# A two-layer trunk in split float32: one 512-column matmul for both activation parts, and the FFN in two sweeps

## The chip, the cores and the metric

The kernel runs on one core of a Trainium2 chip. Its time is the device time of one execution in microseconds. Three runs of the kernel before gave 978.88 us as their median (978.57 to 980.99). The profile comes from one execution, whose span on the core is 975.6 us. Engines are named as in the profile: PE is TensorE, PEld its weight loads, DVE is VectorE, ACT is ScalarE, POOL is GpSimd, SP is SyncE.

## What is computed

A residual stream `h` of 256 tokens and 1,024 channels goes through two layers. Each has a gated FFN (SwiGLU, 2,816 hidden units), a mixer, a second FFN, and a gated per-layer input (PLE). The mixer of layer 0 is a gated linear recurrence over 1,280 channels, that of layer 1 a causal pooling with windows of 2, 4, 8 and 16 tokens. A last norm follows. All is float32:

```python
for i in range(DEPTH):
    h = h + 0.5 * swiglu(rms_norm(h, ffn1_norm[i]), ffn1_w_gate[i], ffn1_w_up[i], ffn1_w_down[i])
    hn = rms_norm(h, mix_norm[i])
    m = rglru_mixer(hn, ...) if i % 2 == 0 else pool_mixer(hn, ...)
    h = h + m
    h = h + 0.5 * swiglu(rms_norm(h, ffn2_norm[i]), ffn2_w_gate[i], ffn2_w_up[i], ffn2_w_down[i])
    gate = jax.nn.sigmoid(rms_norm(h, ple_norm[i]) @ ple_w_gate[i])
    h = h + gate * (p[i] @ ple_w_proj[i])
return rms_norm(h, final_norm)
```

Here `swiglu(x)` is `(silu(x @ w_gate) * (x @ w_up)) @ w_down`.

## The kernel before

**Layout and precision.** Channels lie on partitions, tokens along the free axis. `h` is four tiles of [128, 2, 256], each a pair of channel tiles. The weights come from DRAM as 329 units, [128, 1024] float32 each, in the order in which `stream_order` lists them. A unit holds eight 128x128 blocks; `load` (L251) brings it in on SP's queue, seven units ahead of its use. `split` then makes two fp32r parts of it, `hl`: ScalarE copies the rounded high part (L262) and VectorE subtracts it from the weights for the low part (L263), four units ahead. The activations are split in the same way: `Norm.put` scales `h` by the norm's weights on ScalarE for the high part (L310) and takes the low part on VectorE (L311). Only the gates of the recurrence (`ri`) use float32 itself, which TensorE does in two passes.

**Products.** A product of a weight block `wh + wl` with activations `xh + xl` is three matmuls of 256 columns, all added up in one PSUM region, in `Bank.mm3` (L284 is where `mm` issues them):

```python
def mm3(self, o, wh, wl, xh, xl):
    self.mm(o, wh, xh)
    self.mm(o, wh, xl)
    self.mm(o, wl, xh)
```

The weights are the stationary side, so each of the three has a weight load (PEld). A result for two channel tiles, [128, 2, 256] float32, fills one PSUM bank. There are two PSUM pools of four banks: `gu` for results that are read soon, `acc` for sums that stay.

**Norms.** The norm's scale by token is found beside the products, which don't need it: `rstd_tokens` adds up the squares with matmuls of one column against `ones` (`ss`, L331), VectorE finds 1/sqrt in ten small steps (L341 to L351), `spread` makes two diagonal tiles `dg` (L367) and multiplies them by `ones` (L368) to have the scale on all partitions. ScalarE's squares (L319) are added on GpSimd (L324) before. `project_all` runs several outputs at once, first the lower half of the contraction for each, then the upper half, and places the sums and the spread between its units: `sums_at` and `spread_at` count units from its start.

**An FFN.** The 2,816 hidden units are 11 pairs of tiles, `p`. The first two pairs of gate and up go through `project_all`, four outputs of two units each. Then for every `p` from 2 on: the down products of `p - 2` into four `acc` banks, then gate and up of `p`, 48 matmuls each; so the down products lie between those of gate and up. `evac` reads the gate's bank on VectorE times the scale (L450), takes tanh on ScalarE, multiplies by the up bank (L453, L454), and splits the result into `hid` (L456, L457). At the end every `acc` bank is scaled and added to `h`, and the next norm's `put` follows.

**Around them.** The recurrent mixer projects two branches (`xb`, `gb`) with the same products, in the order of `LRU_FIRST` and `LRU_STEPS`; the step "y1", whose last instruction is `ytp` (L683), has to end before the last products of `lru_out` (`accl`). The pool mixer multiplies tokens by weights (`v`), waits for the norm's scale to split `v` into `vhl`, and multiplies by the pooling matrices (`po`). The PLE projection (`proj`, results `pp`) is written last there and uses the `acc` pool. `keep_warm` (L231) issues products that nobody reads, at the start and before the last spread. The order on each engine is made by the scheduler from the order of the code; `high_priority` blocks come ahead of what is written before them.

## Time and profile before

| | |
|---|---|
| time, median of 3 runs | 978.88 us (978.57 to 980.99) |
| span of the profiled execution | 975.6 us |
| PE busy | 960.1 us, 98% |
| PEld busy | 952.3 us, 98% |
| DVE busy | 652.3 us, 67% |
| ACT busy | 490.8 us, 50% |
| POOL busy | 55.1 us, 6% |
| granted PE clock | at least nine tenths of full in all 40 slices |
| DMA | 173.63 MB, 178 GB/s mean |
| chain that ended last | PE 65%, issue 21%, DVE 9%, ACT 3% |

The profiled execution has no separate time beside its span; the median of the runs stands 3.3 us above that span. Busy times of PE and PEld are those of instructions that overlap each other: a matmul of 256 columns shows 283 ns of duration while the next one starts some 120 ns after it. What one costs is therefore read from the distance of starts, or from a whole stretch and its count. In the chain, one piece is a run of instructions of one line and operand, with its start, its length and how many they are. "Issue" in the chain is time in which an engine waits for nothing that the profile shows.

### The profile page before, as it was taken

Reading aid. Unit: us, or ns where it says so; the run is one execution under the profiler, and the core shown is the slowest. Engines: PE = TensorE matmul, PEld = TensorE weight load, DVE = VectorE, ACT = ScalarE, POOL = GpSimd, SP = SyncE. Lnnn points to the kernel's source line nnn. Section 1 sums busy time; section 2 is a strip of 40 time slices with the busy share of each in tenths; the row PEclk is TensorE's granted clock in tenths of the full one; section 3 lists DMA queues with packets and bytes.
Section 4 is the critical chain, followed back from the end, with each engine's and each line's share of the span. In section 5 each row is a group of like instructions: output and inputs, shape, how many; then the busy total and the mean of one; then the engine's idle time right before and its main releaser. Section 6 shows DMA issues by size and latency. Waiting matters only on the chain.

```text
span 975.6 us, 18712 instructions
## 1 busy us (share of the span) xinstructions
PE 960.1 (98%) x7888; PEld 952.3 (98%) x7888; DVE 652.3 (67%) x853; ACT 490.8 (50%) x634; POOL 55.1 (6%) x48
## 2 busy tenths in 40 slices
PE   9999999999999999999999999999989999999997
PEld 9999999999999999999998999999989999999996
DVE  7956555597977755655579855555679755555685
ACT  7544444468785443544456444444448444434443
POOL 1000000023101000000021000000011000000020
PEclk9999999999999999999999999999999999999999
DMA  8865556554435665566545656565524765655611
GB/s 294 282 213 184 184 178 192 171 177 175 152 108 169 203 203 173 194 193 185 179 123 185 203 180 192 164 204 182 178 95 157 240 192 169 200 189 176 191 45 44
DMA packets 49188, 173.63 MB, mean 178 GB/s; under 512 B 5584, under 2 KB 6224, under 8 KB 49104
## 3 DMA queue, kind: packets, MB, share of 16 engines
q1 hardware_dynamic: 48960, 172.29, 54.7%
q8 instruction: 61, 1.00, 0.4%
q14 instruction: 23, 0.19, 0.1%
q10 hardware_dynamic: 144, 0.15, 0.1%
HBM read 171.37 MB, written 1.05 MB: 177 GB/s over the span
## 4 chain that ended last, share of the span: by engine, by line
PE 65%; issue 21%; DVE 9%; ACT 3%; DMA 0%; POOL 0%; DVEq 0%; ACTq 0%; POOLq 0%
PE up0ffn L284 13%; PE gate0ffn L284 13%; PE acc0ffn L284 12%; PE up1ffn L284 6%; PE gate1ffn L284 6%; PE acc1ffn L284 6%; DVE hl L263 3%; DVE x L311 2%; PE x L284 2%; PE accl L284 1%; PE ri L284 1%; PE ple L284 1%; ACT hl L262 1%; PE b L284 1%; PE xb L284 1%
## 5 line engine op out<-in xcount | busy, mean ns | idle before, releaser
L263 DVE TENSOR_TENSOR hl<-raw,hl 128x1024 fp32r<-128x1024 f32 (+1 forms) x326 | 385.6, 1200 | 238.5 <-ACT hl L262 238.5
L262 ACT ACTIVATE hl<-raw 128x1024 fp32r<-128x1024 f32 (+1 forms) x326 | 331.9, 1035 | 408.3 <-issue 102.5
L284 PE MATMUL gate1ffn<-x,hl 128*128 128x256 f32 x1056 | 132.6, 283 | 2.4 <-DVE x L311 2.4
L284 PE MATMUL gate0ffn<-x,hl 128*128 128x256 f32 x1056 | 132.2, 283 | 0.6 <-ACT hl L262 0.5
L284 PEld LDWEIGHTS gate1ffn<-x,hl 128*128 128x128 f32 x1056 | 128.9, 192 | 3.5 <-DVE x L311 3.2
L284 PE MATMUL up1ffn<-x,hl 128*128 128x256 f32 x1056 | 132.0, 283 | 0.0
L284 PE MATMUL up0ffn<-x,hl 128*128 128x256 f32 x1056 | 131.3, 283 | 0.0
L284 PEld LDWEIGHTS gate0ffn<-x,hl 128*128 128x128 f32 x1056 | 128.8, 192 | 1.3 <-ACT hl L262 0.7
L284 PE MATMUL acc0ffn<-hid,hl 128*128 128x256 f32 x1056 | 129.0, 282 | 0.0
L284 PEld LDWEIGHTS up1ffn<-x,hl 128*128 128x128 f32 x1056 | 128.9, 192 | 0.0
L284 PEld LDWEIGHTS up0ffn<-x,hl 128*128 128x128 f32 x1056 | 128.6, 192 | 0.0
L284 PE MATMUL acc1ffn<-hid,hl 128*128 128x256 f32 x1056 | 128.6, 281 | 0.0
L284 PEld LDWEIGHTS acc0ffn<-hid,hl 128*128 128x128 f32 x1056 | 126.8, 188 | 0.2
L284 PEld LDWEIGHTS acc1ffn<-hid,hl 128*128 128x128 f32 x1056 | 126.8, 188 | 0.0
L324 POOL TENSOR_TENSOR sacc<-sq,sq 128x512 f32<-128x512 f32 x9 | 14.5, 1609 | 838.7 <-ACT sq L319 838.7
L311 DVE SCALAR_TENSOR_TENSOR x<-h,vt,x 128x256 fp32r<-128x256 f32 x64 | 48.8, 802 | 7.0 <-ACT x L310 7.0
L284 PE MATMUL ple<-x,hl 128*128 128x256 f32 x384 | 47.6, 284 | 0.0
L284 PEld LDWEIGHTS ple<-x,hl 128*128 128x128 f32 x384 | 46.5, 192 | 0.2
L456 ACT ACTIVATE hid<-gs 128x512 fp32r<-128x512 f32 x44 | 27.8, 632 | 16.4 <-DVE gs L454 16.3
L310 ACT ACTIVATE x<-h,vt 128x256 fp32r<-128x256 f32 x64 | 28.5, 499 | 5.9 <-DMA vt<-vec 2.7
L454 DVE TENSOR_TENSOR gs<-th,gs 128x512 f32<-128x512 f32 x44 | 30.4, 692 | 1.4
L457 DVE TENSOR_TENSOR hid<-gs,hid 128x512 fp32r<-128x512 f32 x44 | 30.1, 684 | 0.0
(132 smaller groups left out, 683.3 us busy)
## 6 DMA issues: line engine op xcount, KB each, us to landing
raw<-w SPq DMA_DIRECT2D x320, 512.0 KB, 4.2
raw<-w SPq DMA_DIRECT2D x7, 256.0 KB, 4.6
h<-xT SPq DMA_DIRECT2D x4, 256.0 KB, 6.2
out<-hg SPq DMA_DIRECT2D x3, 256.0 KB, 2.8
raw<-w SPq DMA_DIRECT2D x1, 288.0 KB, 2.6
raw<-w SPq DMA_DIRECT2D x2, 128.0 KB, 4.7
out<-hg SPq DMA_DIRECT2D x2, 128.0 KB, 2.0
vt<-vec ACTq DMA_DIRECT2D x1, 148.0 KB, 4.6
```

The source lines that it names most:

```text
L262: nc.scalar.activation(hl[:, 0, c], raw[:, c], AF.Copy)
L263: nc.vector.tensor_tensor(hl[:, 1, c], raw[:, c], hl[:, 0, c].bitcast(F32), op=ALU.subtract)
L284: nc.tensor.matmul(o, lhsT, rhs, start=self.first, stop=self.left == 0, skip_group_check=True)
L310: nc.scalar.activation(xt[:, 0, c], h[:, c], AF.Copy, scale=g)
L311: nc.vector.scalar_tensor_tensor(xt[:, 1, c], h[:, c], g, xt[:, 0, c].bitcast(F32), op0=ALU.mult, op1=ALU.subtract)
L324: nc.gpsimd.tensor_tensor(acc, self.acc, sq, op=ALU.add)
L454: nc.vector.tensor_tensor(gs, th, gs, op=ALU.mult)
L456: nc.scalar.activation(hid[:, 0], gs, AF.Copy)
L457: nc.vector.tensor_tensor(hid[:, 1], gs, hid[:, 0].bitcast(F32), op=ALU.subtract)
```

## The change

**The pair.** A new class `Pair` takes the place of `Bank` for all split products but those of the pool mixer. Its PSUM tile is [128, 2, 2, 256], two banks; for each of the two channel tiles one half is for the high activations and one for the low ones. The high weights meet both activation parts in one matmul of 512 columns, and the low weights meet the high activations in one of 256 columns, which goes into the second half. `join` adds the two halves afterwards: a ScalarE copy of one half and a VectorE addition of the other. The counts: 2,512 products that were three matmuls are now two; 135 joins; VectorE's instructions go from 809 to 946, ScalarE's from 622 to 748.

```diff
-        def mm3(self, o, wh, wl, xh, xl):
-            self.mm(o, wh, xh)
-            self.mm(o, wh, xl)
-            self.mm(o, wl, xh)
+    class Pair:
+        def __init__(self, name, products):
+            self.ps = psum([P, 2, 2, S], name)
+            self.left = [products, products]
+            self.first = [True, True]
+        def mm3(self, m, wh, wl, x):
+            self.left[m] -= 1
+            nc.tensor.matmul(self.ps[:, m, 1], wl, x[:, 0], start=self.first[m], stop=False, skip_group_check=True)
+            nc.tensor.matmul(self.ps[:, m], wh, x, start=False, stop=self.left[m] == 0, skip_group_check=True)
+            self.first[m] = False
+    def join(out, ps, lo):
+        nc.scalar.activation(lo, ps[..., 1, :], AF.Copy)
+        nc.vector.tensor_tensor(out, ps[..., 0, :], lo, op=ALU.add)
```

**PSUM and the norms.** One PSUM pool `ps` of four tiles (two banks each at most) takes the place of the two. `project_all` now has three outputs, since each is a pair; the fourth goes through the new `project_one`, alone. The marks move with it.

```diff
-    gup = ctx.enter_context(tc.tile_pool(name="gu", bufs=4, space=PSUM))
-    accp = ctx.enter_context(tc.tile_pool(name="acc", bufs=4, space=PSUM))
+    pp_ = ctx.enter_context(tc.tile_pool(name="ps", bufs=4, space=PSUM))
...
+    def project_one(key, name, norm, by_tile=False):
+        pair = Pair(name, ND)
+        for kh in range(2):
+            project(pair, unit(*key, kh), kh, norm, by_tile and kh == 1)
+        return pair.ps
-    def project_all(jobs, norm, done, by_tile=False, apart=False, sums_at=3, spread_at=5.5):
+    def project_all(jobs, norm, done, sums_at=3, spread_at=4.5):
...
-    h, norm = ffn(0, "ffn1", h, norm, "mix_norm0", scales, sums_at=4, spread_at=6.5)
+    h, norm = ffn(0, "ffn1", h, norm, "mix_norm0", scales, sums_at=3.5, spread_at=5)
...
-    h, norm = ffn(1, "ffn2", h, norm, "ple_norm1", sums_at=2.5)
+    h, norm = ffn(1, "ffn2", h, norm, "ple_norm1")
```

**The FFN.** All gate and up products come first, for p from 0 to 10; `hid` has a buffer for each p. Then the down products, for the channels' lower half with two accumulating pairs, then for the upper half; the units of the down weights are packed anew for that (256 hidden units by 512 channels).

```diff
+                    join(gs, g, gl)
+                    nc.vector.tensor_tensor(gs, gs, wide(norm.r), op=ALU.mult)
...
+                    join(us, u, ul)
+                    nc.vector.scalar_tensor_tensor(us, th, 1.0, us, op0=ALU.add, op1=ALU.mult)
...
             for p in range(2, NF2):
-                down([part(p - 2)], range(NP_))
                 if middle and p == NF2 // 2:
                     middle()
-                hids[p] = evac(p, gu(p))
+                hids.append(evac(p, *[project_one((which, l, m, p), f"{m}{l}{which}{p}", norm) for m in ("gate", "up")]))
...
+            for d in range(2):
+                accs = [Pair(f"acc{l}{which}{2 * d + j}", 2 * NF2) for j in range(2)]
...
+                for p in range(NF2 - 2):
+                    down([(p, unit(which, l, "down", p, d))], range(2))
+                last = [(p, unit(which, l, "down", p, d)) for p in range(NF2 - 2, NF2)]
+                for j in range(2):
+                    down(last, [j])
```

**The mixers.** In the recurrent layer `LRU_FIRST` loses "b0", which now comes first in `LRU_STEPS`; each branch has a join; the second half of `lru_out` is taken by halves of the channels, so that a pair of channels ends earlier than the next. In the pool layer the four `v` results lie in two tiles of the one PSUM pool, and `proj(1, filler)`, still written last, takes its tiles from there too.

**What stands where now.** Three places, in the order of the instructions on one engine; each line has the instruction's line, operation, out<-in with tile numbers, and shape.

On VectorE, the first FFN's norm: the end of the chain from the sums to the diagonal (`ta`, `tb`, `ty`, then `dg`), with the splits `hl` among its steps. Before:

```order
L347 TENSOR_TENSOR ta1_313<-ty1_312 128x2
L263 TENSOR_TENSOR hl7_279<-raw7_173,hl7_279 128x1024
L348 SCALAR_TENSOR_TENSOR ta1_313<-ta1_313,tms1_311 128x2
L349 TENSOR_SCALAR tb1_314<-ta1_313 128x2
L350 SCALAR_TENSOR_TENSOR tb1_314<-ta1_313,tb1_314 128x2
L263 TENSOR_TENSOR hl8_327<-raw8_219,hl8_327 128x1024
L351 SCALAR_TENSOR_TENSOR ty1_312<-tb1_314,ty1_312 128x2
L367 TENSOR_SCALAR dg1_0_402<-vt_79,ty1_312 128x128
L367 TENSOR_SCALAR dg1_1_405<-vt_79,ty1_312 128x128
```

After:

```order
L373 TENSOR_TENSOR ta1_269<-ty1_268 128x2
L320 TENSOR_TENSOR us0_348<-up0ffn10_205,ul0_349 128x512
L374 SCALAR_TENSOR_TENSOR ta1_269<-ta1_269,tms1_267 128x2
L273 TENSOR_TENSOR hl8_291<-raw8_206,hl8_291 128x1024
L375 TENSOR_SCALAR tb1_270<-ta1_269 128x2
L273 TENSOR_TENSOR hl9_321<-raw9_228,hl9_321 128x1024
L320 TENSOR_TENSOR gs1_400<-gate0ffn11_227,gl1_401 128x512
L376 SCALAR_TENSOR_TENSOR tb1_270<-ta1_269,tb1_270 128x2
L273 TENSOR_TENSOR hl10_360<-raw10_249,hl10_360 128x1024
L377 SCALAR_TENSOR_TENSOR ty1_268<-tb1_270,ty1_268 128x2
L273 TENSOR_TENSOR hl11_381<-raw11_289,hl11_381 128x1024
L393 TENSOR_SCALAR dg1_0_312<-vt_76,ty1_268 128x128
```

The chain's steps are the same; between them stand more splits, and joins (L320) of gate and up.

On TensorE, the pool layer after its norm's sums (`ss`). Before, the projection `pp` and then the pooled products `po`:

```order
L331 MATMUL ss6_8269<-ones_81,sacc6_3_8201 128x1 x4
L284 MATMUL pp1_0_8430<-hl249_8085,hl250_8090 128x256 x6
L284 MATMUL pp1_0_8430<-hl249_8085,hl251_8209 128x256 x6
L284 MATMUL pp1_1_8444<-hl249_8085,hl250_8090 128x256 x6
L284 MATMUL pp1_1_8444<-hl249_8085,hl251_8209 128x256 x6
L284 MATMUL pp1_2_8458<-hl249_8085,hl250_8090 128x256 x6
L284 MATMUL pp1_2_8458<-hl249_8085,hl251_8209 128x256 x6
L284 MATMUL pp1_3_8472<-hl249_8085,hl250_8090 128x256 x6
L284 MATMUL pp1_3_8472<-hl249_8085,hl251_8209 128x256
L284 MATMUL po0_8339<-hl252_8214,vhl00_8290 128x144 x2
```

After, the pooled products follow the sums:

```order
L357 MATMUL ss6_6686<-ones_78,sacc6_3_6620 128x1 x4
L294 MATMUL po0_6756<-hl253_6633,vhl00_6707 128x144
L294 MATMUL po1_6777<-hl253_6633,vhl00_6707 128x144
L294 MATMUL po0_6756<-hl253_6633,vhl00_6707 128x144
L294 MATMUL po0_6756<-hl253_6633,vhl00_6707 128x16
L294 MATMUL po0_6756<-hl254_6721,vhl10_6710 128x128
```

and the projection comes behind the last of them:

```order
L294 MATMUL po3_6823<-hl253_6633,vhl01_6713 128x144 x2
L294 MATMUL po3_6823<-hl253_6633,vhl01_6713 128x16
L294 MATMUL po3_6823<-hl254_6721,vhl11_6716 128x128 x2
L313 MATMUL pp1_0_6847<-hl250_6550,hl251_6555 128x256
L314 MATMUL pp1_0_6847<-hl250_6550,hl251_6555 128x512
L313 MATMUL pp1_0_6847<-hl250_6550,hl251_6555 128x256
```

The projection has moved from ahead of the pooled products to behind them.

On VectorE, one period p = 5 of gate and up in the first FFN. Before (the down products of p = 3 lie beside it on TensorE):

```order
L450 TENSOR_TENSOR gs5_1247<-gate0ffn15_1129,rstd1_400 128x512
L263 TENSOR_TENSOR hl35_1220<-raw35_1130,hl35_1220 128x1024
L263 TENSOR_TENSOR hl36_1258<-raw36_1159,hl36_1258 128x1024
L453 SCALAR_TENSOR_TENSOR th5_1249<-th5_1249,up0ffn15_1188 128x512
L454 TENSOR_TENSOR gs5_1247<-th5_1249,gs5_1247 128x512
L263 TENSOR_TENSOR hl37_1263<-raw37_1189,hl37_1263 128x1024
L457 TENSOR_TENSOR hid5_1253<-gs5_1247,hid5_1253 128x512
```

After:

```order
L320 TENSOR_TENSOR gs5_851<-gate0ffn15_765,gl5_852 128x512
L469 TENSOR_TENSOR gs5_851<-gs5_851,rstd1_310 128x512
L273 TENSOR_TENSOR hl27_832<-raw27_766,hl27_832 128x1024
L273 TENSOR_TENSOR hl28_870<-raw28_787,hl28_870 128x1024
L320 TENSOR_TENSOR us5_858<-up0ffn15_808,ul5_859 128x512
L475 SCALAR_TENSOR_TENSOR us5_858<-th5_856,us5_858 128x512
L273 TENSOR_TENSOR hl29_891<-raw29_809,hl29_891 128x1024
L476 TENSOR_TENSOR gs5_851<-us5_858,gs5_851 128x512
L273 TENSOR_TENSOR hl30_913<-raw30_830,hl30_913 128x1024
L479 TENSOR_TENSOR hid5_864<-gs5_851,hid5_864 128x512
```

VectorE has two joins more per p (L320), and it reads PSUM in them alone; three splits stand in this stretch before, four after.

## Rows read from the trace of the kernel before

**Rows 1.** Page, busy time by engine: engine, busy us, share of the span, instructions.

```profile
PE 960.1 (98%) x7888; PEld 952.3 (98%) x7888; DVE 652.3 (67%) x853; ACT 490.8 (50%) x634; POOL 55.1 (6%) x48
```

**Rows 2.** Chain that ended last, in order of time: start us, us, what.

```profile
55.25 5.75 PE gate0ffn L284 x48
...
66.77 5.70 PE acc0ffn L284 x48
...
223.15 11.23 PE ri L284 x52
```

**Rows 3.** Timeline of PEld: start us, us, engine, line, operation, out<-in, shapes, count.

```profile
280.47 0.30 PEld L284 LDWEIGHTS accl<-yr,hl 128*128 128x128 f32 x2
...
281.49 0.19 PEld L284 LDWEIGHTS accl<-yr,hl 128*128 128x128 f32 x1
...
944.11 0.98 PEld L331 LDWEIGHTS ss<-ones,sacc 128*128 128x128 f32 x8
945.01 4.38 PEld L284 LDWEIGHTS ple<-x,hl 128*128 128x128 f32 x36
```

**Rows 4.** Groups by line: shapes, count | busy, mean ns | idle before, releasers.

```profile
L263 DVE TENSOR_TENSOR hl<-raw,hl 128x1024 fp32r<-128x1024 f32 (+1 forms) x326 | 385.6, 1200 | 238.5 <-ACT hl L262 238.5
L262 ACT ACTIVATE hl<-raw 128x1024 fp32r<-128x1024 f32 (+1 forms) x326 | 331.9, 1035 | 408.3 <-issue 102.5 <-PE acc0ffn L284 62.6 <-PE acc1ffn L284 61.5
...
L454 DVE TENSOR_TENSOR gs<-th,gs 128x512 f32<-128x512 f32 x44 | 30.4, 692 | 1.4
L310 ACT ACTIVATE x<-h,vt 128x256 fp32r<-128x256 f32 x64 | 28.5, 499 | 5.9 <-DMA vt<-vec 2.7 <-DVE h L709 1.9 <-DVE h L544 1.3
L456 ACT ACTIVATE hid<-gs 128x512 fp32r<-128x512 f32 x44 | 27.8, 632 | 16.4 <-DVE gs L454 16.3
...
L324 POOL TENSOR_TENSOR sacc<-sacc,sq 128x512 f32<-128x512 f32 x16 | 24.5, 1531 | 12.1 <-ACT sq L319 11.5
```

**Rows 5.** Window in the first FFN: length, engines' busy us (count), clock, DMA, GB/s.

```profile
55.25:141.32 86.07, 86.07 (x723) 86.07 (x722) 49.23 (x50) 37.02 (x41) 0.00 (x0) 1.00 0.59 185
```

**Rows 6.** Timeline of PE at the start; square brackets: idle before, and releaser.

```profile
0.99 5.17 PE L231 MATMUL idle<-ones 128*128 128x128 f32 x24 [0.99 <-POOL minus L223]
...
19.05 0.95 PE L331 MATMUL ss<-ones,sacc 128*128 128x1 f32 x8
...
27.13 0.60 PE L368 MATMUL spread<-dg,ones 128*128 128x128 f32 x4
```

**Rows 7.** Timeline of DVE in the first norm's chain.

```profile
20.09 0.14 DVE L341 TENSOR_SCALAR tms<-ss 128x2 f32<-128x2 f32 x1
...
25.10 0.48 DVE L367 TENSOR_SCALAR dg<-vt,ty 128x128 f32<-128x128 f32 x2
```

**Rows 8.** Timeline of PE and of DVE in the recurrent layer.

```profile
268.29 11.87 PE L284 MATMUL gb<-x,hl 128*128 128x256 f32 x96
...
292.86 1.49 DVE L683 TENSOR_TENSOR ytp<-xc,yr 128x1280 fp32r<-128x1280 f32 x1
...
294.41 0.38 PE L284 MATMUL accl<-ytp,hl 128*128 128x256 f32 x1 [0.52 <-DVE ytp L683]
```

**Rows 9.** Timeline of PE in the pool layer and at the next FFN's start.

```profile
733.29 5.39 PE L284 MATMUL pp<-hl,hl 128*128 128x256 f32 x43
738.53 4.89 PE L284 MATMUL po<-hl,vhl 128*128 128x144 f32 x40
...
746.96 0.86 PE L284 MATMUL gate1ffn<-x,hl 128*128 128x256 f32 x5 [0.48 <-DVE x L311]
```

**Rows 10.** Timeline of PE in the last PLE.

```profile
950.94 0.68 PE L368 MATMUL spread<-dg,ones 128*128 128x128 f32 x4 [1.35 <-DVE dg L367]
```

**Rows 11.** Timeline of PE at the end; two windows there (columns of rows 5).

```profile
968.18 0.71 PE L368 MATMUL spread<-dg,ones 128*128 128x128 f32 x4
...
966.00:971.50 5.50, 2.80 (x14) 2.03 (x12) 4.47 (x17) 2.08 (x6) 0.00 (x0) 1.00 0.19 63
971.70:975.60 3.90, 0.00 (x0) 0.00 (x0) 0.00 (x0) 0.00 (x0) 0.00 (x0) 0.50 0.52 162
```

More of the change, by code (lines that the diff above doesn't have):

```diff
@@ L227, in keep_warm @@
     def keep_warm(x, n):
[L229 removed]
+        idle = psum([P, x.shape[-1]], "idle")
         for _ in range(n):
@@ L421, in project_all @@
                 if kh == 1:
-                    held.append((i, [b.ps for b in banks[i]] if apart and i == len(jobs) - 1 else banks[i][0].ps))
+                    held.append((i, pairs[i].ps))
                     while held and at + 1 > spread_at:
@@ L458, in evac @@
                 return hid
-            accs = []
-            def down(parts, pairs):
-                if not accs:
-                    accs.extend(bank(accp, "acc", 2 * 2 * NF2 * 3, f"acc{l}{which}{j}") for j in range(NP_))
-                for j in pairs:
-                    for us, hid in parts:
-                        for f, m in [(f, m) for f in range(2) for m in range(2)]:
-                            c = slice((2 * j + m) * P, (2 * j + m + 1) * P)
-                            accs[j].mm3(accs[j].ps[:, m], us[f][:, 0, c], us[f][:, 1, c], hid[:, 0, f], hid[:, 1, f])
-            def part(p):
-                return [unit(which, l, "down", p, f) for f in range(2)], hids.pop(p)
-            hids, first = {}, []
+            hids, first = [], []
             def after_first(i, ps):
@@ L480, in after_first @@
                     nc.vector.tensor_scalar_mul(rq, norm.r, 0.25)
-                if i % 2:
-                    hids[i // 2] = evac(i // 2, first[-2:])
-            project_all([((which, l, m, p), f"{m}{l}{which}{p}") for p in range(2) for m in ("gate", "up")], norm, after_first, **marks)
+                if i == 1:
+                    hids.append(evac(0, *first))
+            project_all([((which, l, m, p), f"{m}{l}{which}{p}") for m, p in (("gate", 0), ("up", 0), ("gate", 1))], norm, after_first, **marks)
@@ L485, in ffn @@
+            hids.append(evac(1, first[2], project_one((which, l, "up", 1), f"up{l}{which}1", norm)))
             for p in range(2, NF2):
-                down([part(p - 2)], range(NP_))
                 if middle and p == NF2 // 2:
                     middle()
-                hids[p] = evac(p, gu(p))
-            before = part(NF2 - 2)
-            down([before], (2, 3, 0))
-            last = part(NF2 - 1)
-            down([last], (0,))
-            down([before, last], (1,))
-            down([last], (2, 3))
@@ L516, in proj @@
         for j in range(NP_):
-            bk = bank(pool, tag, 12, f"pp{l}_{j}")
+            pair = Pair(f"pp{l}_{j}", 2)
             for k in range(2):
@@ L548, in evac @@
                         after.square(j, hj)
-            project_all([(("ple_gate", l, j), f"ple{l}_{j}") for j in range(NP_)], norm, evac, by_tile=True, apart=last, spread_at=4.5 if last else 5.5)
+            project_all([(("ple_gate", l, j), f"ple{l}_{j}") for j in range(NP_ - 1)], norm, evac)
+            evac(NP_ - 1, project_one(("ple_gate", l, NP_ - 1), f"ple{l}_{NP_ - 1}", norm, by_tile=True))
         return new, after
```

207 lines of the change are left out of this document (109 added, 98 removed).

## The prediction

> **What bounds the kernel now.** I read the page's busy times first: TensorE is busy 98% of the 975.6 us span, VectorE 67%, ScalarE 50% [rows 1]. Then the chain that ended last: inside the FFNs it is an unbroken run of gate, up and down matmuls [rows 2]. So a microsecond saved on TensorE counts, as long as the other engines keep up. The question is what one matmul costs there. Two units of a gate are 48 matmuls of 256 columns in 5.75 us, 120 ns each; 48 of the down projection take 5.70 us, 118.75 ns [rows 2]. At 2.4 GHz 256 columns are 106.7 ns, so some 13 ns of each are not columns. Two rows say what they are. The norm's sums stream a single column per matmul, and yet eight weight loads take 945.01 - 944.11 = 0.90 us, 112 ns each; in the output projection nine loads in a row take 281.49 - 280.47 = 1.02 us, 113 ns each, with 256 columns [rows 3]. So a stream of short matmuls is paced by its weight loads, at 112 to 120 ns. The recurrent gates' float32 products show the other side: there a pass of 256 columns is paced at 11.23 us / 52 = 216 ns [rows 2], twice its columns' 106.7 ns and 2.6 ns more. A weight load beside a pass of that length costs next to nothing.
>
> **What the change saves on TensorE.** It turns 2,512 triples (high weights by high part, high by low, low by high: three matmuls of 256 columns, three loads) into pairs (low by high with 256 columns, high by both parts with 512). The columns stay at 768; one load in three goes. No row shows a 512-column matmul. Its bounds are the float32 pass, 216 ns, and 216 + 13 = 229 ns, if every matmul pays the 13 ns that a short one now pays. The short one lies between 113 and 120 ns. So a pair is 329 to 349 ns. I take 216 for the long one, from the row with the same time in the array, and for the short one what each stage shows now, since the load behind it has only 256 columns to hide under, as before:
> - gate and up (1,408 triples), PLE gate (128), PLE projection (32), recurrent inputs (160): 360 - 336 = 24 ns, by 1,728: 41.5 us;
> - down (704): 356.25 - 334.75 = 21.5 ns: 15.1 us;
> - output projection (80): 340 - 329 = 11 ns: 0.9 us.
>
> Together 57.5 us. At 329 ns throughout it would be some 74 us, at 349 some 24.
>
> **What it adds beside TensorE.** Every result now has two halves to join, by a ScalarE copy of one and a VectorE addition, 135 of each. A 128x512 operation is 0.63 us on ScalarE and 0.69 on VectorE [rows 4]: about 85 and 93 us. What hides them? In a steady stretch of an FFN VectorE is now busy 49.2 of 86.1 us [rows 5]. Afterwards gate and up stand by themselves, without the down products that gave VectorE a rest: for each p, 32 pairs are 10.75 us, and VectorE has four splits (4.8 us) and six evacuation steps (4.1 us), 8.9 us; ScalarE has 4 x 1.04 + 4 x 0.63 = 6.7 us [rows 4]. It fits, at 83%. In VectorE's new order the splits stand five units (13 us) ahead of their use, and `hid` has a buffer for each p, so a late evacuation stops nobody. In down VectorE only splits. The SP queue loads the same bytes as now and has room (DMA share 0.59 [rows 5]). So I cost the inside of the FFNs at nothing; the cover is those 1.85 us per p.
>
> **Where the cover is gone**, at the ends of the stages:
> - *First FFN, its norm.* Now 27.13 - 20.00 = 7.1 us of matmuls lie between the sums and their spread, and VectorE needs 25.10 - 20.09 = 5.0 us to the diagonal `dg`, with three splits among its steps [rows 6, 7]. Afterwards 2.5 units (6.7 us) lie there, and the order puts seven splits and three joins into the chain: 5.0 + 4 x 1.2 + 3 x 0.69 = 11.9 us. TensorE waits 5.2 us. The sums also come half a unit earlier, ahead of GpSimd's additions: about 1 us. Sum 6.2 us.
> - *Pool layer.* Between the sums and the pooled products TensorE now does the PLE projection, 738.53 - 733.29 = 5.2 us that cover the norm's chain [rows 9]. One PSUM pool now serves all, the order has the projection behind the pooled products, and those 5.2 us lie open. Behind them it covers some 0.7 us: the wait of 0.48 us for VectorE's scalings at the start of the next FFN [rows 9], and an estimated 0.2 more that the shorter units there would add to it. Sum 4.5 us.
> - *Recurrent layer.* From the end of the last gate product to the last `ytp` is 294.35 - 268.3 = 26.0 us, and TensorE waits 0.5 us for it [rows 8]. Two joins (1.2 us) come into that chain, 27.2 us, while TensorE's work beside it shrinks to 32 x 336 + 40 x 329 ns = 23.9 us: a wait of 3.3 us for 0.5. Sum 2.8 us.
> - *Other boundaries.* The last pair of an FFN goes through copy, join, scale, residual, two scalings, square and GpSimd's sum: 0.63 + 3 x 0.69 + 2 x 0.5 + 0.63 + 1.5 = 5.8 us [rows 4], with some three splits queued between 9.5 us, against three units (8.1 us) that don't need it. So 1.4 us at three places (before the recurrent layer and each PLE gate). At the starts of the other three FFNs splits stand ahead of the norm's chain too, and I take 2, 0.5 and 1 us. The wait of 1.35 us for the last PLE's spread [rows 10] goes, and the tail gets a join and a copy, 0.9 us. Sum 7.3 us.
>
> Together 20.8 us; bounds are 8 us (only the first two, and each smaller) and 32.
> - *The clock.* TensorE's granted clock is full in the window to 971.5 us and half from 971.7, with TensorE idle since 968.9 [rows 11]; at the start 24 passes of 256 cycles took 5.17 us, 215 ns each, twice their time at 2.4 GHz [rows 6]. So a wait of five microseconds may drop it, and the next five run at half: 2.3 us lost. Two waits are that long; I count one drop, between none and two.
>
> **Sum.** 975.6 - 57.5 + 20.8 + 2.3 = 941.2 us of span. The median of the runs stands 3.3 us above the profiled span, so 944.5; I say **944 us**.
>
> **Rivals.**
> - *A, every load at its floor.* If the long matmul lets the short one go at 113 ns everywhere, a pair is 329 ns; with waits of 12 us the time is 978.9 - 74 + 12 = 917. For it: the same shape runs at 113 in one place and at 120 in another. Against: x and its tiles stay as they are, and they are read at 120.
> - *B, each matmul keeps its 13 ns.* A pair is 349 ns: 978.9 - 24 + 23 = 978, no change. Against it: the float32 pass, which keeps 2.6.
> - *C, the excess goes with the columns.* If 256 columns take 120 ns because loads disturb their reading, 512 take 240, a pair is 360 as the triple, and nothing is saved: 978.9 + 23 = 1002, slower. It decides from a long matmul of 216 + (57.5 - 23) / 2.512 = 230 ns upward. Against it: 112 ns with one column. For it: the float32 pass spreads its 256 columns over twice the time, so it is no sure witness. The Trainium skill ("TensorE: Matmul & The Clock Gate", section Back-to-back issue gap) also lets the time go with the columns, N/2.4 plus 2.5 ns when isolated; by that the triple is 327 ns, the pair 325, the saving 6 us and the time near 996. The trace doesn't agree on the triple.
> - *D, VectorE sets the pace of gate and up.* If its order makes it wait for ScalarE by more than 1.85 us per p, each further 0.1 us costs 44 x 0.1 = 4.4 us; a period of 11.5 us gives 944 + 33 = 977, no change. Against it: behind an up product's copy VectorE has four evacuation steps and two splits, 5.2 us, and the next join is due 5.4 us later.
>
> **Chances.** Forecast (930 to 960) 0.53; A 0.22; B 0.10; C 0.08; D 0.07. C is slower; B and D are spread around no change, with their better half faster. 0.3% is about what a measurement of this kernel can tell from no change. Faster 0.84, same 0.05, slower 0.11. The range leaves out C, the worse half of B and of D, and the outer edge of A: 914 to 968.
>
> **What would show it.** In the profile after: pieces of 32 gate or up matmuls in 5.38 us (A 5.26, B 5.58, C 5.76); TensorE idle for VectorE before the first spread, before the pooled products and before the last recurrent product; none inside gate and up, or else D; a granted clock below 1 only behind the two long waits. The forecast fails if the long matmul takes over 230 ns, or if the waits at the ends pass 40 us.

## The result

The changed kernel takes 986.18 us (median of five runs, 983.38 to 987.53), the kernel before 978.57 us (five runs, 977.28 to 980.99). The ratio is 1.007, with a 95% interval of 1.0051 to 1.009: slower by 0.7%, where 944 us and a clear gain were forecast, within 914 to 968.

The profiled execution spans 983.8 us, 8.2 us more than before. Its busy times, from the page, answer to [rows 1]:

```profile
PE 953.9 (97%) x5376; PEld 831.9 (85%) x5376; DVE 733.3 (75%) x989; ACT 561.5 (57%) x761; POOL 53.1 (5%) x48
```

Nearly a third of the weight loads is gone (7,888 to 5,376), and yet TensorE is busy for only 6 us less. VectorE is busy for 81 us more and ScalarE for 71 (93 and 85 were expected from the joins).

**What a pair costs.** The timeline of PE gives the distance of starts. A short matmul (L313) and a long one (L314) make a pair. The first two rows are eight pairs apart in a gate of the first FFN, the next two ten pairs apart in its down products, the last two ten pairs apart in the second layer's first FFN:

```profile
61.51 0.28 PE L313 MATMUL gate0ffn<-x,hl 128*128 128x256 f32 x1
...
64.33 0.28 PE L313 MATMUL gate0ffn<-x,hl 128*128 128x256 f32 x1
...
159.96 0.28 PE L313 MATMUL acc0ffn<-hid,hl 128*128 128x256 f32 x1
...
163.47 0.28 PE L313 MATMUL acc0ffn<-hid,hl 128*128 128x256 f32 x1
...
599.88 0.28 PE L313 MATMUL gate1ffn<-x,hl 128*128 128x256 f32 x1
...
603.34 0.28 PE L313 MATMUL gate1ffn<-x,hl 128*128 128x256 f32 x1
```

That is 2.82 / 8 = 352.5 ns, 3.51 / 10 = 351 ns and 3.46 / 10 = 346 ns, where the forecast had 336, 334.75 and 336. In this execution each stage holds its value throughout: three FFNs have gate and up at 353, the second layer's first FFN at 346.7. The lower value is the sum of a short and a long matmul each in a row of its own kind (first experiment), 346.8. Against the triples of [rows 2] (360 and 356.25 ns) the saving is 1,056 x 7 + 352 x 13.3 ns = 12.1 us on gate and up, 704 x 5.2 = 3.7 on down, some 3 to 4 on the recurrent inputs and the PLE gates. The output projection loses 1.0 (80 pairs at 352.8 ns against triples at 340). Together some 18 us, not 57.5.

**What waits.** The view of waits adds up what TensorE waited for: who waits, for whom, us in total, times, the longest. Before:

```profile
PE v L284 <- DVE x L311: 2.7, 4, 0.8
PE gate1ffn L284 <- DVE x L311: 2.4, 4, 0.7
PE spread L368 <- DVE dg L367: 1.4, 1, 1.4
...
PE accl L284 <- DVE ytp L683: 0.5, 1, 0.5
PE gate0ffn L284 <- ACT hl L262: 0.5, 1, 0.5
```

After:

```profile
PE spread L394 <- DVE dg L393: 6.3, 4, 4.6
PE ss L357 <- POOL sacc L350: 5.2, 6, 3.7
PE po L294 <- ACT vhl L775: 4.3, 1, 4.3
PE accl L313 <- DVE ge L320: 2.0, 1, 2.0
PE v L294 <- ACT x L336: 1.3, 1, 1.3
PE ssf L357 <- ACT sqf L820: 1.1, 1, 1.1
PE accl L314 <- DVE y L705: 1.1, 1, 1.1
PE gate1ffn L314 <- DVE x L337: 1.1, 1, 1.1
```

The sums, without the 1.0 us that both kernels wait at their start, are 7.5 and 22.4 us: 14.9 us of new waits, where 20.8 were forecast. None lies in the steady part of gate, up or down; the 1.1 us of `gate1ffn` stand at an FFN's start, where the kernel before had 2.4.

**What the clock takes.** The granted clock is the third value from the end in these windows (columns of [rows 5]):

```profile
24.00:40.00 16.00, 11.42 (x58) 9.72 (x57) 13.07 (x31) 8.94 (x12) 0.00 (x0) 0.89 0.76 274
544.00:556.00 12.00, 9.68 (x40) 8.53 (x41) 6.02 (x13) 2.26 (x4) 2.26 (x1) 0.72 0.58 197
736.00:756.00 20.00, 15.60 (x66) 14.42 (x66) 17.61 (x36) 13.47 (x26) 4.14 (x3) 0.57 0.25 84
56.00:130.00 74.00, 74.00 (x421) 64.15 (x420) 56.37 (x66) 42.57 (x54) 0.00 (x0) 1.00 0.58 187
```

A window's mean clock falls short of 1 by half the share that ran at half clock. So half clock held for 16 x 0.11 / 0.5 = 3.5 us, 12 x 0.28 / 0.5 = 6.7 us and 20 x 0.43 / 0.5 = 17.2 us, each time at one of the three long waits. The third drop came inside its wait: 17.2 of the 20 us are at half, and the wait of 4.3 us begins with the window. TensorE had work in all but 3 us of the half clock, at about half pace, so some 12 us are lost, an estimate; 2.3 were forecast. The last window is a steady stretch of gate and up: full clock, and TensorE busy in all of its 74 us.

So the result adds up: -18 + 14.9 + 12 = +9 us, against the measured 8.2 of span. By stage, from the starts of the first products in both traces, the first FFN is 3.4 us longer, the recurrent layer 2.1, the second layer's first FFN 1.6, the pool layer 9.2; the two FFNs without a long wait are 2.0 and 4.1 us shorter, the PLEs 0.7 and 2.0; the tail is 0.8 longer.

### The profile page after: what moved, and what is told of

Read it like the earlier page. It is cut to its first block, busy times and chain, and to the rows that moved or that the text cites. A ratio compares the mean times of both kernels' runs of the same rounds, so it can differ in the third digit from the quotient of the medians.

```text
span 983.8 us, 13972 instructions
## 1 busy us (share of the span) xinstructions
PE 953.9 (97%) x5376; PEld 831.9 (85%) x5376; DVE 733.3 (75%) x989; ACT 561.5 (57%) x761; POOL 53.1 (5%) x48
## 4 chain that ended last, share of the span: by engine, by line
PE 82%; DVE 9%; ACT 4%; issue 2%; POOL 1%; DMA 1%; DVEq 0%; ACTq 0%; POOLq 0%
PE acc0ffn L314 8%; PE up1ffn L314 8%; PE acc1ffn L314 8%; PE gate1ffn L314 8%; PE up0ffn L314 8%; PE gate0ffn L314 7%; PE acc0ffn L313 4%; PE acc1ffn L313 4%; PE up1ffn L313 4%; PE gate1ffn L313 4%; PE up0ffn L313 4%; PE gate0ffn L313 4%; DVE hl L273 3%; PE ple L314 2%; PE ri L294 1%
## 5 line engine op out<-in xcount | busy, mean ns | idle before, releaser
L273 DVE TENSOR_TENSOR hl<-raw,hl 128x1024 fp32r<-128x1024 f32 (+2 forms) x327 | 395.0, 1211 | 127.5 <-ACT hl L272 125.3
L272 ACT ACTIVATE hl<-raw 128x1024 fp32r<-128x1024 f32 (+2 forms) x327 | 335.5, 1032 | 169.5 <-PE acc1ffn L314 53.6
L314 PE MATMUL gate1ffn<-x,hl 128*128 128x512 f32 x352 | 126.9, 401 | 1.2 <-DVE x L337 1.1
L314 PE MATMUL up0ffn<-x,hl 128*128 128x512 f32 x352 | 126.7, 402 | 0.0
L314 PE MATMUL gate0ffn<-x,hl 128*128 128x512 f32 x352 | 125.7, 399 | 0.0
L314 PE MATMUL up1ffn<-x,hl 128*128 128x512 f32 x352 | 124.6, 396 | 0.0
L314 PE MATMUL acc0ffn<-hid,hl 128*128 128x512 f32 x352 | 123.7, 393 | 0.0
L314 PE MATMUL acc1ffn<-hid,hl 128*128 128x512 f32 x352 | 123.7, 393 | 0.0
L313 PE MATMUL up0ffn<-x,hl 128*128 128x256 f32 x352 | 99.7, 283 | 0.0
L313 PE MATMUL gate1ffn<-x,hl 128*128 128x256 f32 x352 | 99.6, 283 | 0.0
L313 PE MATMUL acc1ffn<-hid,hl 128*128 128x256 f32 x352 | 99.6, 283 | 0.0
L313 PE MATMUL acc0ffn<-hid,hl 128*128 128x256 f32 x352 | 99.5, 283 | 0.0
L313 PE MATMUL gate0ffn<-x,hl 128*128 128x256 f32 x352 | 99.4, 282 | 0.0
L313 PE MATMUL up1ffn<-x,hl 128*128 128x256 f32 x352 | 99.0, 281 | 0.0
L314 PEld LDWEIGHTS gate1ffn<-x,hl 128*128 128x128 f32 x352 | 67.0, 190 | 17.6 <-DVE x L337 1.8
L314 PEld LDWEIGHTS up0ffn<-x,hl 128*128 128x128 f32 x352 | 66.9, 190 | 16.7
L314 PEld LDWEIGHTS gate0ffn<-x,hl 128*128 128x128 f32 x352 | 66.3, 188 | 16.5 <-DVE x L337 0.3
L314 PEld LDWEIGHTS up1ffn<-x,hl 128*128 128x128 f32 x352 | 66.2, 188 | 15.6
L314 PEld LDWEIGHTS acc0ffn<-hid,hl 128*128 128x128 f32 x352 | 66.1, 188 | 15.3
L314 PEld LDWEIGHTS acc1ffn<-hid,hl 128*128 128x128 f32 x352 | 66.1, 188 | 15.2
L313 PEld LDWEIGHTS gate1ffn<-x,hl 128*128 128x128 f32 x352 | 67.4, 191 | 0.0
L313 PEld LDWEIGHTS up0ffn<-x,hl 128*128 128x128 f32 x352 | 67.3, 191 | 0.0
```

The lines of the kernel that those rows point to most:

```text
L272: nc.scalar.activation(hl[:, 0, c], raw[:, c], AF.Copy)
L273: nc.vector.tensor_tensor(hl[:, 1, c], raw[:, c], hl[:, 0, c].bitcast(F32), op=ALU.subtract)
L313: nc.tensor.matmul(self.ps[:, m, 1], wl, x[:, 0], start=self.first[m], stop=False, skip_group_check=True)
L314: nc.tensor.matmul(self.ps[:, m], wh, x, start=False, stop=self.left[m] == 0, skip_group_check=True)
```

## Experiments

Medians are given with the kernel before on the same chip, which takes 978.1 to 979.9 us there; the changed kernel's 986.18 us stand against 978.57, so differences to it are good to a microsecond or so. Theories: the long matmul is dearer than the float32 pass that stood for it; the waits at the ends of the stages take what is left, with a clock that falls behind them.

One thing bears on the comparisons with the changed kernel. Wherever short and long matmuls alternate, gate and up of an FFN hold one of two paces, 346 or 353 ns a pair, and which of them can differ between kernels that have the same code there. The run with the pool layer's cover put back leaves the first FFN as it is in the changed kernel, and yet the window that has 421 matmuls above has 429 there; by the starts a pair takes 346 ns, for 353:

```profile
56.00:130.00 74.00, 74.00 (x429) 65.27 (x428) 57.83 (x67) 42.75 (x54) 0.00 (x0) 1.00 0.63 192
```

By the starts in the traces, the run with products in a tile of their own and that with later marks have their first and last FFN at the lower pace too, and the run with the last addition on VectorE its first. An FFN's 352 pairs make 2.3 us of it. What sets the pace is not shown, and a gain or loss of 2 to 5 us between two kernels with that order can be this and not the edit. Triples (360) and two by two (348) have one pace in all four FFNs.

### What a stream of matmuls costs by itself

A kernel with no layer of the trunk in it, only streams of 48 (`x2` is 512 columns, `x1` 256), with and without work beside them. Its time is not that of the trunk.

```python
for i in range(N): MM(k[1][:, 0], wt(i), x1, ...)     # L259, short alone
for i in range(N): MM(k[2], wt(i), x2, ...)           # L261, long alone
for i in range(N):                                    # pairs, L263 and L264
    MM(k[3][:, 1], wt(i), x1, ...)
    MM(k[3], wt(i + 1), x2, ...)
for i in range(N // 2): ...                           # two short, two long, L266 to L269
```

> A kernel of streams alone, no layer of the trunk: 48 matmuls in each, weights of 128x128, fp32r where nothing else is said: 256 columns; 512 columns; pairs of both; two short then two long; 128 columns; 512 with one and the same weight block; 512 and 256 in bfloat16; then 512 and pairs beside VectorE and ScalarE at work, and again beside running DMAs. Theory 1 (the excess over the columns' own time goes with the columns, whatever else runs): 512 columns take 230 to 236 ns in every place, a pair 347 to 354, and two short and two long the same per pair. Theory 2 (the excess is a price per weight load): 512 columns 216 to 222 ns, 256 columns 113 to 120, a pair about 335. Theory 3 (the other engines and the DMAs disturb the reading): 512 columns near 214 ns by themselves and 230 to 236 beside them. If weight loads of four bytes are what disturbs, bfloat16 takes 213 to 216 and 107 to 110 ns.

The timeline of PE (a row is a run, with its start, length and count; a stream's pace is the distance to the next stream's start over its count):

```profile
19.83 5.92 PE L259 MATMUL k<-xr,wr 128*128 128x256 f32 x48
25.58 11.07 PE L261 MATMUL k<-xr,wr 128*128 128x512 f32 x48
36.49 0.28 PE L263 MATMUL k<-xr,wr 128*128 128x256 f32 x1
...
53.45 0.28 PE L266 MATMUL k<-xr,wr 128*128 128x256 f32 x1
...
70.17 5.47 PE L271 MATMUL k<-xr,wr 128*128 128x128 f32 x48
...
86.70 10.31 PE L275 MATMUL k<-xb,wb 128*128 128x512 bf16 x47
96.84 5.40 PE L277 MATMUL k<-xb,wb 128*128 128x256 bf16 x48
...
102.00 11.17 PE L285 MATMUL k<-xr,wr 128*128 128x512 f32 x48
113.01 0.28 PE L287 MATMUL k<-xr,wr 128*128 128x256 f32 x1
...
129.97 11.04 PE L293 MATMUL k<-xr,wr 128*128 128x512 f32 x48
140.85 0.28 PE L295 MATMUL k<-xr,wr 128*128 128x256 f32 x1
```

- A short one alone takes 5.75 / 48 = 119.8 ns, a long one alone 10.91 / 48 = 227 ns. Over their columns' 106.7 and 213.3 ns that is 13.1 and 14 ns: the excess goes with the matmul and its load, not with the columns. (Which of the two takes it, no run separates: with one and the same weight block, loaded anew each time, a long one takes 229 ns.) This is the price that rival B had, and it stands against 216 ns. At 128 columns (L271) the distance is 110.6 ns, as the 112 of [rows 3] with one column: there the loads seem to set the pace. At 512 columns they can't, and the excess is as large as at 256.
- One after the other, short and long take (53.45 - 36.49) / 48 = 353.3 ns, 6.5 ns more than 119.8 + 227 = 346.8. Two short and then two long take (70.17 - 53.45) / 48 = 348.3 ns.
- Beside VectorE and ScalarE at work the long one takes (113.01 - 102.00) / 48 = 229.4 ns (L285) and a pair (129.97 - 113.01) / 48 = 353.3 (L287). In the next long stream, whose second half has DMAs beside it, the long one takes (140.85 - 129.97) / 48 = 226.7 (L293), and the pairs behind it (L295), at a DMA share of 0.80, again 353.3 by their starts. Theory 3 falls.
- In bfloat16 a long one takes 10.14 / 47 = 215.7 ns (47 recorded starts). A short one takes (5.40 - 0.27) / 47 = 109.1, from the row's length less one matmul's 0.27 us, since the stream behind it starts early. Over their columns that is 2.4 ns in both. The price belongs to these four-byte streams, at full rate; the float32 pass, which spreads its columns over twice the time, doesn't pay it.

### The pair undone

```diff
-            nc.tensor.matmul(self.ps[:, m], wh, x, start=False, stop=self.left[m] == 0, ...)
+            nc.tensor.matmul(self.ps[:, m, 1], wh, x[:, 1], start=False, stop=False, ...)
+            nc.tensor.matmul(self.ps[:, m, 0], wh, x[:, 0], start=False, stop=self.left[m] == 0, ...)
```

> The changed kernel with one part undone: the pair is three matmuls of 256 columns again (low by high and high by low into one half, high by high into the other), with all else as changed: joins, PSUM tiles, FFN in two sweeps, marks. By the measured steps (a pair at 346.7 to 353 ns, a triple at 356 to 360) the pair is worth 12 + 4 + 3 = some 18 us, so 1002 to 1007 us. By the forecast (57.5 us) it would be about 1043 us. If the pair is worth nothing, 986 us.

1,001.84 us (before: 978.09). The pair is worth 1,001.84 - 986.18 = 15.7 us, a little under what the measured steps say, and not the forecast's 57.5. The other reading of this run: all that the change adds beside the pair (joins, PSUM tiles, the new orders, with the waits and the clock that they bring) costs 1,001.84 - 978.09 = 23.8 us. The forecast's sum for it was 20.8 + 2.3 = 23.1.

### Two short, then two long

```diff
         def mm3(self, m, wh, wl, x):
+            self.held.append((m, wh, wl, x))
+            if len(self.held) < 2:
+                return
+            for m, wh, wl, x in self.held:     # the short ones
...
+            for m, wh, wl, x in self.held:     # the long ones
```

> The changed kernel with its matmuls in another order: two short ones, then the two long ones of the same two products, in place of short, long, short, long. Nothing else differs. Theory 1 (a load costs some 13.5 ns, and each change between a short and a long matmul 6 ns more in the stages at 353 ns; the streams alone gave 353.4 alternating and 348.3 by two and two): 1,056 gate and up pairs at 353 lose 5 ns each, the down products 2 to 3, the stage at 346.7 stays: 5 + 2 + 1 = some 8 us less, 976 to 980 us, with gate and up at 348 ns a pair. Rival (the order of the streams is beside the point, the stages at 353 differ by where their tiles lie): 984 to 987 us.

981.37 us (before: 979.78; ratio 1.0016, 1.0006 to 1.0025), some 5 us less than the changed kernel and a microsecond above the range that was expected. In the timeline twelve products, six groups of two, stand between these two rows of gate and up, or 4.18 / 12 = 348.3 ns:

```profile
61.09 0.40 PE L317 MATMUL gate0ffn<-x,hl 128*128 128x256 f32 x2
...
65.27 0.40 PE L317 MATMUL gate0ffn<-x,hl 128*128 128x256 f32 x2
```

Every FFN now has 348, the one that was at 346.7 too: the order takes away the difference between the FFNs. It doesn't show what made it.

### Products that nobody reads, to hold the clock

```diff
+            for _ in range(ahead):       # eight ahead of the sums, in the second layer's first FFN
+                nc.tensor.matmul(both[:, 1, 0], ones, vt[:, 0:S], start=True, stop=True)
             self.token_sums(ps, ...)
+            for _ in range(behind):      # nine behind the sums, in the pool layer
+                nc.tensor.matmul(both[:, 1, 0], ones, self.acc[:, 0], start=True, stop=True)
```

> The changed kernel with products that nobody reads in two waits of TensorE: nine behind the pool layer's sums, and eight ahead of the sums of the second layer's first FFN. The waits stay, only the clock can change. Theory 1 (the two waits drop the granted clock, and the work behind them runs at half: 14 and 6.5 us of it) gives back 7 + 3 = 10 us: 975 to 978 us, with the clock at 1.00 behind both. Rival (the waits themselves are the whole cost, the clock costs nothing): 986 us.

984.47 us (983.54 to 991.07; before 978.09): nothing clear was gained, and the run says little on the clock. VectorE read the sums only when the products behind them in the same PSUM tile (L388) had ended, as its timeline shows:

```profile
743.91 0.16 DVE L367 TENSOR_SCALAR tms<-ss 128x2 f32<-128x2 f32 x1 [2.90 <-PE ss L388]
```

So the way from the sums to the pooled products grew from 4.3 to 6.8 us by what was meant to fill it, and the products were put into a tile of their own, in the pool layer alone:

```diff
             norm.rstd_tokens()
+            keep_warm(norm.acc[:, 0], 9)
```

> The changed kernel with nine products that nobody reads behind the pool layer's sums, in a PSUM tile of their own (in the earlier run they lay in the sums' tile, and VectorE waited for them); the results v are grouped so that the first pooled products wait for one tile alone. Theory 1 (the clock falls because TensorE idles, and the 14 us behind the wait run at half): the wait is filled, the granted clock stays at 1.00 from the sums to the next FFN, 6 to 7 us less: 977 to 981 us. Rival (the clock falls whatever TensorE does there, or it is worth nothing): 984 to 987 us.

984.15 us (981.14 to 987.72; before 979.78), within the rival's span. The timeline of PE and three windows show why:

```profile
735.48 6.14 PE L241 MATMUL idle<-sacc,ones 128*128 128x256 f32 x18
754.88 0.39 PE L313 MATMUL gate1ffn<-x,hl 128*128 128x256 f32 x1 [2.94 <-DVE pp L320]
...
727.80:734.50 6.70, 4.52 (x30) 4.12 (x28) 3.32 (x6) 3.96 (x9) 1.65 (x2) 0.87 0.41 139
734.50:740.00 5.50, 5.50 (x18) 4.64 (x18) 3.29 (x13) 3.18 (x7) 0.00 (x0) 0.54 0.35 110
740.00:756.00 16.00, 13.06 (x86) 11.55 (x85) 14.78 (x25) 12.46 (x22) 4.16 (x3) 1.00 0.20 66
```

The wait ahead of the pooled products is filled, and half clock holds for 6.7 x 0.13 / 0.5 + 5.5 x 0.46 / 0.5 = 6.8 us instead of 17.2. At full clock the pooled products take 5.0 us, where the run before had 9.2. But the clock still fell, at 732.7, 2 us behind a wait of 2 us ahead of `v` that the new grouping of `v` made longer, and TensorE, now sooner through, waits 2.94 us at the next FFN's start, for VectorE. A faster stretch ran into the next late engine: from the first `v` to the next FFN the layer is 0.5 us shorter, and the first and the last FFN, at the lower pace, give more than that.

### The pool layer's cover put back

The results `v` are grouped here as in the run above.

```diff
             filler = proj_units(1)
+            proj_early(1, filler)       # two of the four outputs, three matmuls each, into one PSUM tile
...
-            proj(1, filler)
+            proj(1, filler, (2, 3))
```

> The changed kernel with the pool layer's cover put back: the first half of the PLE projection (as three matmuls of 256 columns into one PSUM tile) stands between the sums and the pooled products, the second half behind them. Theory 1 (the projection's move laid the norm's chain open, and the wait dropped the clock): the wait of 4.6 us shrinks below 1 us and the 14 us behind it run at the full clock, 4 + 7 = 11 us less: 974 to 977 us. Rival (the wait was VectorE's own, longer chain, and stays): 984 to 987 us.

980.36 us (977.91 to 983.91; before 978.09; ratio 1.0024, 1.0009 to 1.004): some 6 us less than the changed kernel, about half of what was expected. In the profiled executions the pool layer goes from 30.5 to 27.3 us, 3.2 less; the first and the last FFN, now at the lower pace, give 4.6, and the edit doesn't touch them.

```profile
729.16 4.28 PE L294 MATMUL v<-hl,x 128*128 128x256 f32 x18 [2.03 <-ACT x L336]
...
736.53 1.70 PE L294 MATMUL pp<-hl,hl 128*128 128x256 f32 x12 [0.68 <-ACT pp L547]
738.62 0.33 PE L294 MATMUL po<-hl,vhl 128*128 128x144 f32 x1 [0.39 <-ACT vhl L791]
```

The wait of 4.3 us is gone; 0.7 us ahead of `pp` and three pieces of some 0.4 ahead of `po` are left. So the cover was real. What remains of the layer's length is again the wait ahead of `v` (2.0 us), and half clock: 3.4 us behind that wait and 6.8 us from 743.7 on.

### Later marks

```diff
-    h, norm = ffn(1, "ffn1", h, norm, "mix_norm1")
+    h, norm = ffn(1, "ffn1", h, norm, "mix_norm1", sums_at=4, spread_at=5.5)
```

and the first FFN's `spread_at` from 5 to 5.5.

> The changed kernel with the norm's marks later in two FFNs: the first FFN's spread half a unit later (5.5), and the second layer's first FFN's sums a unit later (4) and its spread at 5.5. Theory 1 (both waits are VectorE's and GpSimd's chains laid open, TensorE only stands in the wrong place): the first spread's wait goes from 4.7 to 3.3 us, that of the sums from 3.8 to about 1, and the clock drop behind it goes, 3 us: 6 to 7 us less in all, 977 to 981 us. Rival (the wait only moves to the spread, which now stands 1.5 units behind the sums, 4.2 us for a chain of 5 or more): 984 to 987 us.

985.13 us (981.92 to 986.71; before 979.78): the rival's span. The first FFN's spread waits 4.6 us as before, half a unit later. The second layer's sums stand a unit later, and wait 3.4 us for 3.7, because GpSimd's last addition has become longer. The timelines of POOL, of the kernel before, of the changed kernel, and of this one:

```profile
537.38 1.48 POOL L324 TENSOR_TENSOR sacc<-sacc,sq 128x512 f32<-128x512 f32 x1 [2.49 <-ACT sq L319]
```

```profile
543.69 2.58 POOL L350 TENSOR_TENSOR sacc<-sacc,sq 128x512 f32<-128x512 f32 x1 [6.36 <-ACT sq L345]
```

```profile
543.39 4.84 POOL L350 TENSOR_TENSOR sacc<-sacc,sq 128x512 f32<-128x512 f32 x1 [6.37 <-ACT sq L345]
```

And what VectorE does there in this run:

```profile
543.63 3.48 DVE L273 TENSOR_TENSOR hl<-raw,hl 128x1024 fp32r<-128x1024 f32 x3
```

Three splits of together 3.48 us lie within the addition's 4.84, and the difference is 1.36 us, an undisturbed addition. In the changed kernel one split of 1.2 us and 2.58 - 1.2 = 1.38 us give the same. GpSimd seems to stand still while a split runs. The Trainium skill ("SBUF — State Buffer", section Who interferes with whom) says that a VectorE instruction with two inputs in SBUF contends with GpSimd's reads over a shared port, and calls that sharing an exclusive lock; these rows agree. The split is not the whole of the changed kernel's wait of 3.7 us: TensorE stands from 542.6, and the addition starts at 543.69, since the residual that it needs is late. Without the split some 2.5 us would be left, by these rows.

### The last addition on VectorE

```diff
-                nc.gpsimd.tensor_tensor(acc, self.acc, sq, op=ALU.add)
+                (nc.vector if j == NP_ - 1 else nc.gpsimd).tensor_tensor(acc, self.acc, sq, op=ALU.add)
```

> The changed kernel with the last addition of each norm's squares on VectorE in place of GpSimd. Theory 1 (GpSimd stands still while VectorE runs a split: its last addition took 2.58 us beside one split and 4.84 beside three, against 1.3 to 1.5 before): the sums of the second layer's first FFN wait under 1.5 us instead of 3.8, the clock drop behind them goes (3 us), and the three waits of 0.6 us ahead of other sums go: 5 to 7 us less, 978 to 981 us. Rival (the addition is late because the residual itself is late): 984 to 987 us.

978.97 us (974.72 to 983.62; before 979.93; ratio 0.9993, 0.9974 to 1.0011): 7 us less than the changed kernel. The wait of 3.7 us ahead of the sums falls to 1.6, the short ones ahead of other sums go. One wait moves: the spread behind them waits 1.7 us, 1.1 more. So not all of the 7 us is the edit's: the profiled execution is 5.5 us shorter, 2.6 of it in that FFN; the first FFN has the lower pace here (2.3 us) and a longer stretch of half clock.

### Streams in larger groups, and GpSimd beside splits

A kernel of streams alone, with no layer of the trunk.

```python
for i in range(4): g.tensor_tensor(q[0], q[0], q[1], ...)                       # L276, GpSimd alone
for i in range(10): nc.vector.tensor_tensor(big[:, 1], big[:, 0], w32[:, 1], ...)   # L281, splits
for i in range(8): g.tensor_tensor(q[0], q[0], q[2], ...)                       # L283, beside them
```

> A kernel of streams alone, no layer of the trunk: pairs one by one, four short and four long, eight and eight; then GpSimd's additions of 128x512 by themselves, beside VectorE's splits (128x1024, both operands in SBUF), and beside VectorE's joins (one operand in PSUM). Theory 1 (a price per load of 13 to 14 ns and one per change of length): 353 ns a pair one by one, 347 to 348 by fours and eights. Rival (the pair's price is that of the rows it reads): 353 in all. On GpSimd, theory 1 (it stands still while VectorE reads two operands from SBUF): one addition takes 1.3 to 1.5 us alone, and ten splits lengthen those beside them by 11 to 12 us together; beside joins 1.3 to 1.5 again. Rival (it only shares bandwidth): every addition takes up to 2 us beside both.

```profile
37.64 0.64 PE L263 MATMUL k<-xr,wr 128*128 128x256 f32 x4
...
53.08 0.63 PE L263 MATMUL k<-xr,wr 128*128 128x256 f32 x4
...
54.48 1.12 PE L268 MATMUL k<-xr,wr 128*128 128x256 f32 x8
...
68.45 1.12 PE L268 MATMUL k<-xr,wr 128*128 128x256 f32 x8
```

Eleven groups of four give 15.44 / 44 = 350.9 ns a pair, five groups of eight 13.97 / 40 = 349.3. Larger groups gain nothing over two by two. A price for each change of length would have given 347 to 348 here, so that part of theory 1 doesn't hold; the 13 to 14 ns of each matmul stay. On GpSimd and VectorE, from their timelines:

```profile
13.70 5.38 POOL L276 TENSOR_TENSOR q<-q,q 128x512 f32<-128x512 f32 x4 [11.02 <-ACT q L273]
19.41 17.40 POOL L283 TENSOR_TENSOR q<-q,q 128x512 f32<-128x512 f32 x8 [0.34 <-DVE go L278]
...
20.09 20.33 DVE L281 TENSOR_TENSOR big<-big,w 128x1024 f32<-128x1024 f32 x10
```

Alone an addition takes 1.35 us; beside splits 2.18, and a split 2.03 where the trunk has 1.2 [rows 4]. Eight additions and ten splits would be 10.8 + 12 = 22.8 us one after the other, and both were done after 21.0: they nearly take turns. Here both gave way, in the trunk GpSimd alone. The joins came too late to stand beside any addition, so whether a join disturbs GpSimd stays open.

### The parts together

Two short and two long, the cover in the pool layer, and the later marks:

> The three together on the changed kernel: two short and two long, the pool layer's cover, the later marks. If the parts add up (8, 6 and 6 us less than 986), 964 to 968 us, faster than the kernel before by 1%. If the waits only move, 974 to 980 us, the same as before.

975.67 us (before: 979.78; ratio 0.9958, 0.9945 to 0.997). By the medians the parts alone gave 5, 6 and 1 us, with the two paces in the second and the third; together they give 10.5, half of the 20 expected, with the sums' wait still there. Then with the last addition on VectorE, `sums_at=3.5`, the first spread back at 5, and nine products that nobody reads ahead of that spread, in the spread's PSUM tile:

```diff
         def spread(self, y, ahead=0):
+            both = psum([P, 2, 2, S], f"spread{self.sid}")
+            ps = both[:, 0, 0]
+            for _ in range(ahead):
+                nc.tensor.matmul(both[:, 1, 0], ones, vt[:, 0:S], start=True, stop=True)
```

> The changed kernel with two short and two long matmuls, the pool layer's cover, the last addition on VectorE, the second layer's first FFN's sums half a unit later, and nine products that nobody reads ahead of the first spread. The three together gave 975.7 us with the wait of 3.7 us ahead of those sums and its clock drop still there; without them 4 to 6 us less, and 1 to 3 less where the clock stays at 1.00 behind the first spread: 967 to 971 us, 1% below the kernel before. If the waits move to the spreads: 973 to 977 us.

969.20 us (before: 979.93; ratio 0.9899, 0.9884 to 0.9914): 17 us less than the changed kernel and 1% faster than the kernel before. The window at the first spread, of the version before and of this one:

```profile
24.00:40.00 16.00, 11.39 (x55) 9.73 (x55) 12.73 (x31) 8.46 (x12) 0.00 (x0) 0.79 0.84 298
```

```profile
24.00:40.00 16.00, 16.00 (x93) 14.05 (x93) 14.76 (x25) 9.73 (x13) 0.00 (x0) 1.00 0.87 284
```

The nine products shorten no chain. But the clock stays full behind them, where it was at half for 16 x 0.21 / 0.5 = 6.7 us, and 93 records of matmuls stand in the same 16 us where 55 stood; the first FFN is 3.5 us shorter. This is the clean look at the clock that the two earlier runs were meant to give, though a part of the 3.5 us is that of the addition and the marks.

## Why the prediction was wrong

- **What bounds the kernel** was right: TensorE, its pace by matmul and load.
- **The pair's price** was the step that failed. The sum put the long matmul at 216 ns, "from the row with the same time in the array", a float32 pass. Measured alone it takes 227, and one by one with short ones some 236, which is over the 230 at which the text itself said that the forecast fails. The pair is 346.7 to 353 ns, for 329 to 336. The text named the weak point itself, under rival C ("it is no sure witness"), and bounded the long matmul at 229; with 229 everywhere the pair would have been 349 and the time 978. So rival B's mechanism is what happened, 13 ns for each matmul and its load, with up to 6.5 ns on top where short and long alternate, which no row of before could show. A pace set by the loads, as the text had it for short matmuls, fits 128 columns (110.6 ns), but not the same excess at 256 and 512. The term measured 15.7 to 18 us, for 57.5.
- **Rival C** had the right sign and the wrong mechanism: the excess doesn't grow with the columns (13.1 ns at 256, 14 at 512). The formula of the Trainium skill ("TensorE: Matmul & The Clock Gate", section Back-to-back issue gap) is met by the bfloat16 streams (215.7 ns for 512 columns, 109.1 for 256), not by these.
- **The inside of the FFNs at nothing** was right: no wait there, and rival D (VectorE sets the pace) didn't happen.
- **The waits** were forecast as 20.8 us and came to 14.9. The first norm has 4.6 + 0.5 us for 6.2, the pool layer 4.3 for 4.5, the recurrent layer 2.0 + 1.1 - 0.5 = 2.6 for 2.8. "Other boundaries" came short in all but one place, for which the text had at most 2 us, as a matter of splits: the 3.7 us ahead of the second layer's sums, where the residual is late and a split draws out GpSimd's addition by 1.2 us.
- **The clock** was the second term that was mis-sized: 12 us for 2.3. The text counted one drop of five microseconds at half; there were three, and one held for 17 us. Its own [rows 11] had the clock at half 2.8 us after TensorE's last product, so waits under five microseconds were in question too. The 12 us are those of one execution: a wait of 2.0 us ahead of `accl` left the clock full here, and in the runs with later marks and with the addition on VectorE half clock followed the same wait for 3.4 us.
- **Sum.** With the measured terms the forecast's own sum is 975.6 - 18 + 14.9 + 12 = 984.5, for a measured span of 983.8. The added cost as a whole was right, 23.8 us by the run without the pair for 23.1 forecast, though waits and clock shared it otherwise.

## What to carry to other kernels

The price of a shape that no row shows should be taken from streams of that very shape, type and order, or its range left as wide as the nearest rows: here some 16 ns on a pair, 11 of them the long matmul's alone, times 2,512, were the whole sign. A change that thins out an engine at its bound makes every chain beside it later by comparison, so a small saving per instruction has to be set against each place where work used to stand as cover. And behind each wait of some microseconds the clock may take as much again as the wait did.

## What the runs showed of the hardware

- An fp32r matmul of this kernel costs some 13 to 14 ns over its columns' time, whether it has 256 columns or 512; in bfloat16 2.4 ns. At 128 columns it takes 110.6 ns. Work of VectorE, ScalarE or the DMAs beside them leaves a pair at 353.3 ns.
- Short and long ones in turn cost 6.5 ns a pair more than each in a row in a stream by itself, two by two 1.5, four by four 4.1 and eight by eight 2.5 ns. In the FFNs the order in turn ran at 346 or at 353 ns, the same code at either in different kernels; what sets it stays open.
- GpSimd's additions and VectorE's splits hinder each other: 4.84 us for an addition beside three splits, 1.48 beside none; in a long mix 2.18 us for an addition and 2.03 for a split.
- Half clock lasted 3.5, 6.7 and 17.2 us at three waits of 3.7 to 4.6 us, with TensorE busy through most of it. The same wait of 2.0 us was followed by half clock in some kernels and not in others.
